# FFN input projection by a seven-product block scheme, with each engine's work in a written order

## The chip, the cores and the metric

The kernel runs on one NeuronCore of a Trainium2 chip. Five engines run side by side, each with its own instruction queue: TensorE (PE in the profile; its weight loads are listed as PEld), VectorE (DVE), ScalarE (ACT), GpSimd (POOL) and SyncE (SP, which here only issues transfers). TensorE multiplies a stationary 128x128 block with a moving block of up to 512 columns and writes to PSUM, which has 8 banks of 128x512 floats. Everything else lies in SBUF. [...]

The metric is device time in microseconds of one execution. A profiled execution gives the trace; its span runs from the first to the last instruction.

## What is computed

One decoder layer on 512 tokens with model width 1024: a hybrid mixer (short gated convolution, stick-breaking attention, a chunked state-space scan, merged by gates), then a SwiGLU FFN with hidden width 2816. Both have a pre-norm conditioned by `c`, and a post-norm with a gate. The part that is changed is the product with `w_ffn_in`:

```
x  = x + gate1 * RMSNorm_post(mixer(h))
h2 = rms_norm(x, g_pre_ffn) * (1 + scale2) + shift2      # 512 x 1024
gt, up = split(h2 @ w_ffn_in, 2)                         # w_ffn_in: 1024 x 5632
f  = (silu(gt) * up) @ w_ffn_out                         # w_ffn_out: 2816 x 1024
x  = x + gate2 * RMSNorm_post(f)
```

All inputs and the output are float32.

## The kernel before

Every large product is done in three matmuls on two parts: an operand is cast to a high part on ACT, and DVE subtracts it from the original to get the low part (`split`, lines 146 to 148; in the profile L147 is the cast, L148 the subtraction). `mm3` (lines 150 to 153) then adds high x high, high x low and low x high into one PSUM bank.

Weights come through a common queue. `chunks` lists all weight blocks of the program in their order of use; `load_chunk` loads the next one on the SP queue into one of three 1 MB tiles (tag `wraw`), and `split_piece` splits 128x1024 of it into a high tile `whi` and a low tile `wlo`, of which there are four each. One such split is a "piece". `piece()` (line 212) hands out piece i and, before that, emits the splits up to piece i+2 (`LOOK = 3`). So the split of a piece stands two pieces ahead of its use in the instruction order.

The program runs through these stages. A start stage makes the modulation and the first projection columns. Then TensorE goes through the mixer's projections, with generators for attention, scan and modulation rows pumped between the pieces. Mixer tiles come from one pool of 41 buffers of 128x512 floats (tag `t2`). Then the output projection `w_o` in two passes of two token blocks each; behind each block `x1_chain` (lines 986 to 1009) does the post-norm, the residual sum and the next pre-norm, and `h2_tiles` transposes the result on TensorE and splits it into `h2h` and `h2l` (8 row blocks of 128 by 512 tokens).

FFN-in (lines 1041 to 1073) goes over 22 blocks of 128 hidden columns, each with a gate half and an up half. A half is one piece: 8 row blocks x 3 matmuls of 512 tokens into one bank. The first four halves are done for tokens 0 to 255 first, while the chain of the last two token blocks still runs, then for tokens 256 to 511. After each block `sigm` (three ACT operations: exp, log, exp) and two DVE products give f, which is split into `fh` and `fl` at once. FFN-out then goes over the 11 pairs of hidden blocks, twice, once for each half of the output columns.

The order of instructions is left to a scheduler outside the start stage; inside a `tc.manual_schedule` block the named engines do their work in the order in which it is written.

The lines that the steps of the prediction touch are `piece` and `split_piece` (weights), lines 1049 to 1073 (FFN-in), 1086 to 1106 (FFN-out) and the tile pools.

## Time and profile before

| | us |
|---|---|
| median of 3 runs (802.52 to 804.99) | 802.79 |
| profiled execution | 804.18 |
| its span | 802.5 |
| TensorE busy | 772.6 |
| DVE busy | 460.8 |
| ACT busy | 376.0 |
| POOL busy | 134.8 |

The difference between the profiled execution and its span is what lies before the first and after the last instruction. Busy times of matmuls overlap in the trace, since they are pipelined: the time that a matmul really takes in a stream is the distance from one start to the next. The clock that the throttle granted to TensorE was full throughout (mean 0.999). In a line of the groups, the columns after the bar are the busy time of the group, the mean duration of one instruction in nanoseconds, and the idle time just before its instructions with what ended it. In a table of stretches each line has the stretch, its length, then busy time and instruction count of PE, PEld, DVE, ACT and POOL, the granted clock, the DMA share and GB/s. FFN-in begins at 426.3 us of the span, FFN-out at 672.9.

### The profile page before, as it was taken

To read this page: it belongs to the slowest core of one execution; us is meant where nothing else is said; L and a number is where in the kernel's file an instruction comes from. 1 tells how busy PE (TensorE), PEld (TensorE's weight loads), DVE (VectorE), ACT (ScalarE), POOL (GpSimd) and SP (SyncE) were. 2 spreads that over 40 slices of the span, in tenths; PEclk is the share of its full clock that TensorE was granted. 3 is DMA by queue.
4 is the path that set the end of the run, shared out by engine and by line. 5 is a ranking of instruction groups with operands and counts; after the bars stand their busy time and mean duration, and the time that the engine had idled before them with its cause. 6 is when DMAs were issued, how large, how long until landed. Compare 5 with 4: busy or idle time off the path is not lost.

```text
span 802.5 us, 9537 instructions
## 1 busy us (share of the span) xinstructions
PE 772.6 (96%) x3661; PEld 631.4 (79%) x3661; DVE 460.8 (57%) x667; ACT 376.0 (47%) x623; POOL 134.8 (17%) x175
## 2 busy tenths in 40 slices
PE   3899999999999999999999999999999999999997
PEld 2679887767678888888778988888888888888886
DVE  5999968568847566545698534434434346323214
ACT  5566544566667374551565634434434444213112
POOL 4453412345520100202133000000000000000000
PEclk9999999999999999999999999999999999999999
DMA  9981441122416686755754332222233345532102
GB/s 281 299 261 55 128 135 53 53 81 94 141 56 203 213 237 208 212 182 121 273 187 129 105 99 70 96 94 72 97 105 105 105 158 186 180 108 92 39 1 105
DMA packets 90525, 108.71 MB, mean 135 GB/s; under 512 B 3244, under 2 KB 69856, under 8 KB 90480
## 3 DMA queue, kind: packets, MB, share of 16 engines
q1 hardware_dynamic: 86128, 99.62, 38.7%
q0 software_dynamic: 3584, 7.42, 4.3%
q10 hardware_dynamic: 768, 1.07, 0.4%
q8 instruction: 28, 0.46, 0.2%
q14 instruction: 17, 0.14, 0.1%
HBM read 102.33 MB, written 2.10 MB: 130 GB/s over the span
## 4 chain that ended last, share of the span: by engine, by line
PE 46%; DVE 4%; issue 1%; ACT 1%; DMA 1%; DVEq 0%; ACTq 0%; POOLq 0%
PE pfg L152 5%; PE pfu L152 5%; PE pfu L151 5%; PE pfg L151 5%; PE pfu L153 4%; PE pfg L153 4%; PE pfo L153 4%; PE pfo L152 4%; PE pfo L151 4%; DVE wlo L148 2%; DVE t2k L997 1%; DVE x L999 1%; DMA gate<-gate 1%; DVE st L1004 1%; PE pf L151 1%
## 5 line engine op out<-in xcount | busy, mean ns | idle before, releaser
L147 ACT CAST whi<-wraw 128x1024 fp32r<-128x1024 f32 (+1 forms) x133 | 137.2, 1035 | 262.0 <-PE pfg L152 76.4
L148 DVE TENSOR_TENSOR wlo<-wraw,whi 128x1024 fp32r<-128x1024 f32 (+1 forms) x133 | 164.9, 1243 | 155.6 <-ACT whi L147 155.1
L152 PE MATMUL pgt<-hl,whi 128*128 128x512 f32 x192 | 75.7, 394 | 0.0
L153 PE MATMUL pgt<-hh,wlo 128*128 128x512 f32 x192 | 75.5, 393 | 0.0
L151 PE MATMUL pgt<-hh,whi 128*128 128x512 f32 x192 | 75.4, 393 | 0.0
L152 PE MATMUL pfg<-h2l,whi 128*128 128x512 f32 x160 | 63.0, 394 | 0.0
L152 PE MATMUL pfu<-h2l,whi 128*128 128x512 f32 x160 | 63.0, 394 | 0.0
L151 PE MATMUL pfg<-h2h,whi 128*128 128x512 f32 x160 | 62.7, 392 | 0.0
L151 PE MATMUL pfu<-h2h,whi 128*128 128x512 f32 x160 | 62.7, 392 | 0.0
L153 PE MATMUL pfu<-h2h,wlo 128*128 128x512 f32 x160 | 62.1, 388 | 0.0
L153 PE MATMUL pfg<-h2h,wlo 128*128 128x512 f32 x160 | 62.1, 388 | 0.0
L152 PE MATMUL pfo<-wlo,fh 128*128 128x512 f32 x154 | 60.8, 395 | 0.0
L153 PE MATMUL pfo<-whi,fl 128*128 128x512 f32 x154 | 60.8, 395 | 0.0
L151 PE MATMUL pfo<-whi,fh 128*128 128x512 f32 x154 | 60.7, 394 | 0.0
L923 POOL DMA_DIRECT2D macc<-in_mod_b_dram x8 | 6.8, 849 | 288.6 <-DVE macc L917 241.5
L917 DVE SCALAR_TENSOR_TENSOR macc<-wraw,sc,macc 128x512 f32<-128x512 f32 x56 | 44.2, 789 | 12.1 <-DMA wraw<-in_mod_w_dram 5.5
L151 PEld LDWEIGHTS pgt<-hh,whi 128*128 128x128 f32 x192 | 36.1, 188 | 8.4 <-issue 0.4
L152 PEld LDWEIGHTS pgt<-hl,whi 128*128 128x128 f32 x192 | 36.1, 188 | 8.1
L153 PEld LDWEIGHTS pgt<-hh,wlo 128*128 128x128 f32 x192 | 36.1, 188 | 7.9
L151 PEld LDWEIGHTS pfu<-h2h,whi 128*128 128x128 f32 x160 | 30.0, 188 | 7.0
L151 PEld LDWEIGHTS pfg<-h2h,whi 128*128 128x128 f32 x160 | 30.0, 188 | 7.0
L153 PEld LDWEIGHTS pfu<-h2h,wlo 128*128 128x128 f32 x160 | 30.0, 188 | 6.7
(360 smaller groups left out, 1668.8 us busy)
## 6 DMA issues: line engine op xcount, KB each, us to landing
wraw<-in_w_ffn_in_dram SPq DMA_DIRECT2D x22, 1024.0 KB, 5.0
wraw<-in_w_in_dram SPq DMA_DIRECT2D x20, 1024.0 KB, 5.2
wraw<-in_mod_w_dram SPq DMA_DIRECT2D x16, 1024.0 KB, 5.2
wraw<-in_w_ffn_out_dram SPq DMA_DIRECT2D x10, 1024.0 KB, 4.9
wraw<-in_mod_w_dram SPq DMA_DIRECT2D x16, 512.0 KB, 6.6
wraw<-in_w_o_dram SPq DMA_DIRECT2D x8, 1024.0 KB, 5.6
gate<-gate POOLq DMA_DIRECT2D x14, 256.0 KB, 4.2
xn<-in_x_dram SPq DMA_DIRECT2D x8, 256.0 KB, 5.0
```

The costliest lines, as they stand in the source:

```text
L147: act.copy(hi, src)
L148: vec.tensor_tensor(lo, src, hi.bitcast(F32), ALU.subtract)
L151: pe.matmul(o, whi, xhi, start=start, stop=False)
L152: pe.matmul(o, whi, xlo, start=False, stop=False)
L153: pe.matmul(o, wlo, xhi, start=False, stop=stop)
L917: vec.scalar_tensor_tensor(acc, mw[:, r], c_, acc, op0=ALU.mult, op1=ALU.add)
L923: nc.gpsimd.dma_start(acc[0:1, :], mod_b[n0:n0 + 512].unsqueeze(0), accum_op=ALU.add)
L997: vec.scalar_tensor_tensor(t_, pos[hf], st[:, 2:3], G1[hf], op0=ALU.mult, op1=ALU.mult)
L999: vec.tensor_tensor(xv, xv, t_, ALU.add)
L1004: vec.tensor_tensor(st[:, 3:4], st[:, 3:4], st[:, 4:5], ALU.add)
```

## The change

FFN-in is done on blocks. The 1024 inner rows are cut in two halves, the tokens in two halves (0 to 255, 256 to 511), and two neighbouring hidden blocks form a unit, of which there are 11. That gives a 2x2 by 2x2 block product, which is computed in seven block products ("steps" 1 to 7) in place of eight. A step multiplies one 512-row, two-halves-wide weight block (gate and up, a piece of 128x1024) with 256 tokens: 2 x 4 x 3 = 24 matmuls of 256 columns. Steps 1 and 2 use weight blocks of the first hidden block with the two inner halves of tokens 0 to 255; steps 7 and 4 use blocks of the second hidden block with token differences; steps 5, 6 and 3 use weight sums. Step 2 adds onto the bank of step 1, step 3 onto that of step 5.

- Weight sums: one DVE sum (`wsum`) and two accumulating DMAs on POOL's queue for the steps 5, 6 and 3, and a third accumulating DMA that changes the weight block of step 7 in place. Each moves 512 KB from SBUF to SBUF.
- Token sums T1 to T4 and their splits are made once, between the steps of the first two units, whose steps are interleaved (1 1 2 2 5 5 6 6 7 7 4 4 3 3). The other nine units go 5 1 4 6 7 2 3.
- Results are combined on DVE and ACT: a copy of step 1's bank, one sum after step 6, three operations `c2` after step 7, one sum in `third_of` after step 3; then the sigmoids and products. The products of a sigmoid are put off to the next step (`later`, `flush`).
- TensorE, DVE and ACT do all this in the written order.
- f is kept unsplit; only unit 0 is split inside FFN-in, unit 1 at its end, the others inside the first half of FFN-out, two units ahead of their use.
- The weights of FFN-in come in columns of 128 (runs of 512 bytes, before 1 KB), into four tiles: the three of before and one more that lies in the memory of the closed mixer pool.
- The pool `t2` shrinks from 41 to 30 buffers. A new pool of 12 buffers (`q2`) holds the branch results of attention and convolution (`ybh`, `ybl`, `yah`, `yal`), the scan's `cbm`, later the rows `SH` and `SC` and the normalised `xm`, and in FFN-in the split token sums `tx`.

```diff
-NT2 = 41
+NT2 = 30
...
+    tq = tqs.enter_context(tc.tile_pool(name="tq", bufs=1, side="right"))
+
+    def q2(name, dt=F32):
+        return tq.tile([P, 512], dt, tag="q2", name=name, bufs=12)
...
+    NU = MF // 2
+    WINO = [(u, q) for q in (1, 2, 5, 6, 7, 4, 3) for u in range(2)]
+    WINO += [(u, q) for u in range(2, NU) for q in (5, 1, 4, 6, 7, 2, 3)]
+    units = {}
+    late_pool = {}
+
+    def wino_load(u, i):
+        at["wino"] = at.get("wino", 0) + 1
+        if at["wino"] % 4:
+            raw = raw_tile()
+        else:
+            raw = late_pool["fp"].tile([P, 2048], F32, tag="raw4", name="wraw", bufs=1)
+        raw = raw.rearrange("p (g k n) -> p g k n", g=2, k=8)
+        for g in range(2):
+            c0 = g * FFN + (2 * u + i) * P
+            nc.sync.dma_start(raw[:, g], w_ffn_in[:, c0:c0 + P].rearrange(
+                "(k p) n -> p k n", k=8))
+        units[u][i] = [raw[:, :, 4 * a:4 * a + 4].rearrange("p g k n -> p g (k n)")
+                       for a in range(2)]
+
+    def wino_piece(u, q):
+        if u not in units:
+            units[u] = {}
+            for i in range(1 if u == 1 else 2):
+                wino_load(u, i)
+        un = units[u]
+        if q == 5:
+            un["s"] = late_pool["fx"].tile([P, 2, 512], F32, tag="wsum", name="wsum", bufs=2)
+            vec.tensor_tensor(un["s"], un[1][0], un[1][1], ALU.add)
+            nc.gpsimd.dma_start(un[1][0], un[0][0], accum_op=ALU.add)
+        src = {1: (0, 0), 2: (0, 1), 4: (1, 1), 7: (1, 0)}.get(q)
+        src = un[src[0]][src[1]] if src else un["s"]
+        hi = wp.tile([P, 1024], FR, tag="whi", name="whi").rearrange("p (g n) -> p g n", g=2)
+        lo = wp.tile([P, 1024], FR, tag="wlo", name="wlo").rearrange("p (g n) -> p g n", g=2)
+        split(hi, lo, src)
+        if q in (5, 6):
+            nc.gpsimd.dma_start(un["s"], un[0][q - 5], accum_op=ALU.add)
+        return [t_.rearrange("p g (k n) -> p g k n", k=4) for t_ in (hi, lo)]
...
-    for mp in range(MF // 2):
-        chunks.append(("cols", [[(0, KD, w_ffn_in[:, o + mp * 256:o + (mp + 1) * 256])]
-                                for o in (0, FFN)], 256, 2))
+    chunks.append(("wino", WINO, 0, 1))
...
-    pf = {}
-    fw = {}
-    for i in range(4):
-        pf[i], fw[i] = bank("pf"), piece()
-        ffn_mm(pf[i], fw[i], lo_t, True, False)
-        if i == 2:
-            h2_tiles(*todo.pop(0))
-    h2_tiles(*todo.pop(0))
...
-        if m < 2:
-            pg, pu = pf[2 * m], pf[2 * m + 1]
-        else:
-            pg, pu = bank("pfg"), bank("pfu")
-            for pt in (pg, pu):
-                ffn_mm(pt, piece(), all_t, True, True)
-        f = fq.tile([P, T], F32, tag="f", name="f")
-        sigm(f, pg)
-        vec.tensor_tensor(f, f, pg, ALU.mult)
-        vec.tensor_tensor(f, f, pu, ALU.mult)
-        split(fh[:, m, :], fl[:, m, :], f)
...
+    fp = ctx.enter_context(tc.tile_pool(name="fp", bufs=1, reuse_waits="tile"))
+    fxs = ExitStack()
+    fx = fxs.enter_context(tc.tile_pool(name="fx", bufs=1, reuse_waits="tile"))
+    late_pool.update(fp=fp, fx=fx)
+    wino_load(1, 1)
...
+    def flush():
+        while later:
+            later.pop(0)()
+    def step(q, o, start, stop):
+        hi, lo = piece()
+        flush()
+        for g in range(2):
+            cs = slice(g * 256, g * 256 + 256)
+            for k in range(4):
+                if q in tb_of:
+                    xh, xl = hbh[:, tb_of[q], k, :], hbl[:, tb_of[q], k, :]
+                else:
+                    xh, xl = (t_[k // 2][:, k % 2, :] for t_ in tx[q])
+                for part, (a_, b_) in enumerate(((hi, xh), (hi, xl), (lo, xh))):
+                    pe.matmul(o[:, cs], a_[:, g, k, :], b_,
+                              start=(start and g + k + part == 0),
+                              stop=(stop and k == 3 and part == 2), skip_group_check=True)
+    def gated(dst, g, u, sg):
+        sigm(sg, g)
+        def products():
+            vec.tensor_tensor(dst, sg, g, ALU.mult)
+            vec.tensor_tensor(dst, dst, u, ALU.mult)
+        later.append(products)
...
+    def gated_m1(f4, p4, p5, p7, u2):
+        c2 = two(temp("c2", 1024))
+        vec.tensor_tensor(c2[:, 0, :], p7, u2, ALU.add)
+        vec.scalar_tensor_tensor(c2[:, 1, :], p5, -1.0, c2[:, 0, :], op0=ALU.mult,
+                                 op1=ALU.subtract)
+        vec.tensor_tensor(c2[:, 0, :], p4, c2[:, 0, :], ALU.subtract)
+        gated(two(f4[:, 1, :]), c2[:, :, 0:256], c2[:, :, 256:512], two(temp("sg1", 512)))
+    def third_of(f4, p5, u2):
+        vec.tensor_tensor(u2, p5, u2, ALU.add)
+        gated_m0(f4, u2, 1)
...
+    with tc.manual_schedule(engines={ET.PE, ET.DVE, ET.Activation}):
+        pb_ = {1: [], 5: [], 6: [], 7: [], 4: []}
+
+        def fresh(q):
+            pb_[q].append(bank(f"pf{q}"))
+            step(q, pb_[q][-1], True, True)
+        u2s = [temp("u2", 512, 2) for _ in range(2)]
+        for u in range(2):
+            fresh(1)
+            act.copy(u2s[u], pb_[1][u])
+        for u in range(2):
+            step(2, pb_[1][u], False, True)
+            pts[u] = h2_tr(*todo.pop(0))
+
+        t1_, b22, t2_, t3_, t4_ = (f4_tile(n) for n in ("t1r", "b22", "t2r", "t3r", "t4r"))
+
+        def k4(t_, u):
+            return t_[:, u, :].rearrange("p (k t) -> p k t", k=4)
+
+        def parts_of(q, t_, u):
+            for k0 in (0, 2):
+                ts = slice(u * P, (u + 1) * P)
+                h_, l_ = (t__[k0 // 2][:, :, ts] for t__ in tx[q])
+                split(h_, l_, k4(t_, u)[:, k0:k0 + 2, :])
+        for q in (6, 7, 4):
+            tx[q] = [[q2("tx", FR).rearrange("p (k t) -> p k t", k=2) for _ in range(2)]
+                     for _ in range(2)]
+        tks = [slice(u * P, (u + 1) * P) for u in range(2)]
+        for u in range(2):
+            vec.tensor_tensor(k4(t1_, u), hbh[:, 0, :, tks[u]].bitcast(F32), pts[u][0],
+                              ALU.subtract)
+            vec.tensor_tensor(k4(t1_, u), k4(t1_, u), hbl[:, 0, :, tks[u]].bitcast(F32), ALU.add)
+            split(hbh[:, 3, :, tks[u]], hbl[:, 3, :, tks[u]], k4(t1_, u))
+            act.copy(k4(b22, u), pts[u][1])
+        for u in range(2):
+            vec.scalar_tensor_tensor(k4(t2_, u), k4(t1_, u), -1.0, k4(b22, u), op0=ALU.mult,
+                                     op1=ALU.subtract)
+            parts_of(6, t2_, u)
+        for u in range(2):
+            f4s.append(f4_tile("f4"))
+            gated_m0(f4s[u], pb_[1][u], 0)
+            flush()
+        fresh(5)
+        fresh(5)
+        for u in range(2):
+            vec.tensor_tensor(k4(t3_, u), k4(b22, u), pts[u][0], ALU.subtract)
+            parts_of(7, t3_, u)
+        for u in range(2):
+            fresh(6)
+            vec.tensor_tensor(u2s[u], pb_[6][u], u2s[u], ALU.add)
+        for u in range(2):
+            vec.tensor_tensor(k4(t4_, u), hbh[:, 1, :, tks[u]].bitcast(F32), k4(t2_, u), ALU.add)
+            vec.tensor_tensor(k4(t4_, u), k4(t4_, u), hbl[:, 1, :, tks[u]].bitcast(F32), ALU.add)
+            parts_of(4, t4_, u)
+            split(hbh[:, 2, :, tks[u]], hbl[:, 2, :, tks[u]], k4(b22, u))
+        fresh(7)
+        fresh(7)
+        for u in range(2):
+            fresh(4)
+            gated_m1(f4s[u], pb_[4][u], pb_[5][u], pb_[7][u], u2s[u])
+        for u in range(2):
+            step(3, pb_[5][u], False, True)
+            third_of(f4s[u], pb_[5][u], u2s[u])
+        for u in range(2, NU):
+            f4s.append(f4_tile("f4"))
+            p5 = bank("pf5")
+            step(5, p5, True, True)
+            p1, u2 = bank("pf1"), temp("u2", 512, 2)
+            step(1, p1, True, True)
+            act.copy(u2, p1)
+            p4 = bank("pf4")
+            step(4, p4, True, True)
+            p6 = bank("pf6")
+            step(6, p6, True, True)
+            vec.tensor_tensor(u2, p6, u2, ALU.add)
+            p7 = bank("pf7")
+            step(7, p7, True, True)
+            gated_m1(f4s[u], p4, p5, p7, u2)
+            step(2, p1, False, True)
+            gated_m0(f4s[u], p1, 0)
+            if u == NU - 1:
+                t_ = fp.tile([P, 2, 2, T], FR, tag="raw4", name="fparts", bufs=1)
+                f_parts(0, (t_[:, 0], t_[:, 1]))
+            step(3, p5, False, True)
+            third_of(f4s[u], p5, u2)
+        flush()
+    fxs.close()
+    tqs.close()
+    fo = ctx.enter_context(tc.tile_pool(name="fo", bufs=1, reuse_waits="tile"))
+
+    def f_split(u):
+
+        f_parts(u, [fo.tile([P, 2, T], FR, tag="f4o", name="fparts", bufs=10) if u < 6
+                    else f4_tile("fparts", FR) for _ in range(2)])
+    f_split(1)
...
             w = piece()
+            if hf == 0:
+                f_split(i + 2)
```

84 lines of the change are left out of this document (53 added, 31 removed).

## The prediction

> **What bounds the kernel now.** I read the page first: busy shares, the row of slices, the granted clock, the chain that ended last.
>
> ```profile
> PE 772.6 (96%) x3661; PEld 631.4 (79%) x3661; DVE 460.8 (57%) x667; ACT 376.0 (47%) x623; POOL 134.8 (17%) x175
> ...
> PE   3899999999999999999999999999999999999997
> ...
> PEclk9999999999999999999999999999999999999999
> ...
> PE 46%; DVE 4%; issue 1%; ACT 1%; DMA 1%; DVEq 0%; ACTq 0%; POOLq 0%
> ```
>
> TensorE is full from the second slice to the last at an unthrottled clock, and the chain runs through it. So matmul columns are the currency, and a change that removes columns gains as long as VectorE (DVE) and ScalarE (ACT) still deliver operands in time. The second view is the table of stretches: the two mixer stretches, then the start of FFN-in, its steady part, and the first half of FFN-out.
>
> ```profile
> 45.00:200.00 155.00, 152.00 (x779) 123.44 (x778) 123.62 (x215) 91.47 (x167) 62.31 (x90) 1.00 0.33 103
> 200.00:380.00 180.00, 178.37 (x795) 142.79 (x794) 110.08 (x145) 95.99 (x147) 33.30 (x37) 1.00 0.59 176
> ...
> 426.30:453.20 26.90, 25.56 (x210) 24.61 (x209) 20.48 (x26) 15.34 (x34) 6.31 (x4) 1.00 0.25 79
> 453.20:672.90 219.70, 219.70 (x962) 180.30 (x961) 93.32 (x107) 90.40 (x122) 0.82 (x1) 1.00 0.34 110
> 672.90:738.00 65.10, 65.10 (x280) 52.20 (x280) 26.53 (x33) 17.66 (x25) 1.97 (x3) 1.00 0.38 120
> ```
>
> FFN-in is 426.3 to 672.9, 246.6 us. Its steady part is 960 matmuls of 512 columns in 219.7 us, 0.2289 us each, with DVE busy 93 and ACT 90: both wait for TensorE. One pair of hidden blocks (a "unit" below, 96 such matmuls) costs 21.97 us.
>
> **TensorE work removed.** The seven products need 11 units x 7 steps x 24 = 1848 matmuls of 256 columns. The start of FFN-in already has that shape, from the timeline:
>
> ```profile
> 446.27 0.28 PE L153 MATMUL pf<-h2h,wlo 128*128 128x256 f32 x1
> ...
> 447.21 0.28 PE L152 MATMUL pf<-h2l,whi 128*128 128x256 f32 x1
> ```
>
> Eight intervals lie between these starts: 0.94/8 = 0.1175 us each, slightly over half of 0.2289. A step is 2.82 us, a unit 19.74, all 1848 matmuls 217.1. Today's are 219.7 + 192 x 0.1175 = 242.3. TensorE alone would save 25.2 us. The matmul record of 0.28 us says that a result lands 0.16 us behind the issue.
>
> **What the other engines get.** The page's groups by shape, DVE first:
>
> ```profile
> L148 DVE TENSOR_TENSOR wlo<-wraw,whi 128x1024 fp32r<-128x1024 f32 x129 | 161.7, 1256 | 155.6 <-ACT whi L147 155.1 <-PE pk L153 0.4
> L1071 DVE TENSOR_TENSOR f<-f,pfg 128x512 f32<-128x512 f32 x20 | 13.8, 689 | 17.0 <-ACT f L159 17.0
> L774 DVE TENSOR_TENSOR ce<-ce,xs 128x256 f32<-128x256 f32 x8 | 3.3, 411 | 0.0
> L147 ACT CAST whi<-wraw 128x1024 fp32r<-128x1024 f32 x129 | 134.8, 1048 | 262.0 <-PE pfg L152 76.4 <-PE pfu L152 48.0 <-PE pfo3b L153 31.0
> L158 ACT ACTIVATE f<-f,one_c 128x512 f32<-128x512 f32 x22 | 15.9, 724 | 0.7
> L159 ACT ACTIVATE f<-f 128x512 f32<-128x512 f32 x22 | 13.9, 632 | 0.7
> L157 ACT ACTIVATE f<-pfg 128x512 f32<-128x512 f32 x20 | 11.9, 593 | 0.0
> L585 ACT ACTIVATE sb_e<-sb_e,one_c 128x256 f32<-128x256 f32 x2 | 1.0, 506 | 0.0
> L584 ACT ACTIVATE sb_e<-sb_e 128x256 f32<-128x256 f32 x2 | 0.8, 416 | 0.0
> L583 ACT ACTIVATE sb_e<-pz 128x256 f32<-128x256 f32 x2 | 0.8, 384 | 0.0
> L280 ACT CAST wxh<-wxr 128x256 fp32r<-128x256 f32 x8 | 3.2, 400 | 1.0 <-DMA wxr<-in_w_in_dram 1.0
> ```
>
> Per unit DVE gets seven weight subtractions and one weight sum (8 x 1.26), seven operations of 512 (7 x 0.69) and four of 256 (4 x 0.41): 16.5 us, against four subtractions and six of 512, 9.2 us, in 21.97 now. ACT gets seven casts (7.3), one copy (0.6), a sigmoid of 512 (0.59 + 0.72 + 0.63 = 1.95) and two of 256 (0.38 + 0.51 + 0.42 = 1.31 each): 12.5 us. DVE would be at 84% of a 19.74 us unit. That fits as a sum, but the order is fixed on both engines, and ACT and DVE feed each other: cast, then subtraction; PSUM sum on DVE, then sigmoid on ACT, then products on DVE. So I follow the cycle of waits.
>
> How far instructions of one engine overlap, and what a hand-over costs, from the timeline:
>
> ```profile
> 387.28 4.72 DVE L148 TENSOR_TENSOR wlo<-wraw,whi 128x1024 fp32r<-128x1024 f32 x4
> ...
> 461.02 0.63 ACT L159 ACTIVATE f<-f 128x512 f32<-128x512 f32 x1
> ...
> 461.69 0.69 DVE L1071 TENSOR_TENSOR f<-f,pfg 128x512 f32<-128x512 f32 x1 [0.69 <-ACT f L159]
> ```
>
> Four subtractions take 4.72 instead of 5.02, and a hand-over is 461.69 - 461.65 = 0.04.
>
> **Steady unit (steps 5, 1, 4, 6, 7, 2, 3).**
> - Loop part 1, from the last matmul of step 7 to the split of the next unit's piece 5. On DVE the three c2 operations (2.07); behind them on ACT the sigmoid of 512 (1.95), and only then the cast of piece 5 (1.05); then its subtraction (1.26). With 0.16 of drain and four hand-overs 6.65 us. TensorE has steps 2 and 3 meanwhile plus the two matmuls that need no low part, 5.88. It waits 0.8.
> - Part 2, from there to the split of piece 4. DVE does two products of 512, the subtraction of piece 1, two products of 256 and the sum of third_of, 4.15. ACT can cast piece 4 only behind third_of's sigmoid (1.31 + 1.05), then the subtraction (1.26); with hand-overs 7.89. TensorE has the rest of step 5, step 1 and two matmuls, 5.65. It waits 2.2.
> - Part 3: the rest of step 4, steps 6 and 7, 8.23 of pure TensorE.
>
> The loop is 22.8, less about 0.4 for overlap on DVE: 22.4 us, already 0.4 above today's unit.
>
> The third accumulating DMA can lengthen it. It may start only once piece 6 is split, 2.08 after part 2 (two products, one subtraction); after it come cast and subtraction of piece 3 (2.43 with hand-overs), and the c2 operations stand behind that subtraction on DVE. So a landing time D is free up to 8.39 - 4.51 = 3.9 us. No transfer of 512 KB from SBUF to SBUF is in the trace; the nearest are these, the second of them giving minimum, median and maximum:
>
> ```profile
> gate<-gate POOLq DMA_DIRECT2D x14, 256.0 KB, 4.2
> ...
> DMA to landing us min/median/max: 3.3/4.2/7.1
> ...
> wraw<-in_w_ffn_out_dram SPq DMA_DIRECT2D x10, 1024.0 KB, 4.9
> ...
> wraw<-in_w_ffn_out_dram SPq DMA_DIRECT2D x2, 512.0 KB, 4.1
> ```
>
> Bounds for D are 3.3 (the fastest of half the size) and 8.4 (twice the median). Doubling a load adds 0.8; for an accumulation, which reads its target too, I take 1.0 and D = 5.2, nearest to the median row. That adds 1.3: a unit of 23.7. Nine units against 21.97: +15.6 us; with D at its ends +4 and +44.
>
> [...]
>
> **The first two units.** They interleave (1 1 2 2 5 5 6 6 7 7 4 4 3 3), and the token sums T1 to T4 are formed on the way. Step 5 waits for the last transposes, which the x1 chain sets:
>
> ```profile
> 440.22 1.32 PE L1015 MATMUL pt<-ident,xm 128*128 128x128 f32 x8 [1.32 <-DVE xm L1007]
> ...
> 441.55 0.74 PE L151 MATMUL pf<-h2h,whi 128*128 128x256 f32 x4
> ```
>
> From 441.55 TensorE has ten steps, 28.2 us. DVE has some 30 operations of 512, 20 of 256 and nine of 1024: 20.7 + 8.2 + 11.3 = 40.2. It also stands for the casts of T1 and of every second part (about 3.6) and for two sigmoids that share one buffer (2.6). So this part is bound by DVE: about 46.4 after 441.55, or 61.7 after 426.3, against 26.9 + 21.97 = 48.9 now: +12.8. Its bounds: 0 (full overlap, T1 of the first half done earlier, no waits: 33.5) and +18 (another 5 us if the piece-5 splits wait for the x1 chain on DVE or for the fourth weight tile, which lies in memory of the closed pool).
>
> **What I cost at nothing.** In FFN-out ten splits of 1024 columns come in, 12.6 on DVE and 10.5 on ACT; in its first half they are busy 26.5 and 17.7 of 65.1 us, so TensorE covers them; without cover the first one costs up to 2 us. The last unit needs no next piece 5, which I leave in. The weight loads are the same bytes in shorter runs, at a DMA share of 0.34. In the mixer 12 long-lived tiles leave a pool that shrinks by 11; TensorE idles 3.0 + 1.6 us there now, and I take 0, within 3 either way.
>
> **Sum.** +15.6 + 12.8 = +28.4. The profiled execution took 804.18 us (span 802.5, 1.7 around it); the median of the runs is 802.79, 1.4 lower. Forecast 804.2 + 28.4 = 832.6 on its scale, 831 on the median's. Its own range is +4 to +62, 807 to 865.
>
> **Rivals.**
> - The queues keep up everywhere and TensorE stays the bound: -25.2, 778. For it: both engines have slack as sums. Against it: parts 1 and 2 are chains of single instructions, each with a row. Chance 0.14.
> - Only the start stalls and the steady units run at 19.74: 12.8 - 9 x 2.23 = -7.3, 795. It needs piece 5 split 3 us sooner than I find. Chance 0.11.
> - The accumulating DMAs collide with the 1 MB loads that the freed tiles start: D = 8.4, 44 + 12.8 = +57, 860. The maximum of 7.1 for half the size speaks for it; the third DMA mostly falling ahead of the loads speaks against. It decides from D = 3.9 on. Chance 0.11.
> - The mixer loses more to its smaller pool than FFN-in changes by: if its idle of 4.6 us tripled, +9 on the forecast, 840. Chance 0.04.
> - My forecast: 0.60.
>
> Below 0.3% (2.4 us) a change cannot be told from none here. Faster gets the first two rivals: 0.24, a little less for their upper edge; same 0.07 from the edges where gains and stalls cancel; slower 0.69. The range 784 to 857 leaves out about half of each outer rival and the forecast's thin top.
>
> **What would show it.** A steady unit of 22 to 25 us between the starts of its step 5, with TensorE idle before steps 5 and 4, released by wlo or whi; DVE above 65% in FFN-in; casts of wsum waiting for a DMA; the two first units ending near 488. If TensorE is solid from 450 on and a unit is 19.7, I am wrong in parts 1 and 2; if whi waits for the accumulation by over 3 us, D was too small.

## The result, and the profile after

The changed kernel takes 869.53 us (median; 867.97 to 870.63) against 802.79 (802.52 to 804.99): a ratio of 1.0823, with a 95% interval of 1.0798 to 1.0849. The forecast was 831 with a range of 784 to 857. The sign was right, the size was not: 28.4 us were forecast and 66.7 came, above the range.

First the page of the changed kernel: busy shares, TensorE's slices and granted clock, and the chain that ended last, by engine and by line.

```profile
PE 779.5 (90%) x4357; PEld 664.8 (77%) x4357; DVE 558.7 (64%) x801; ACT 421.6 (49%) x703; POOL 173.0 (20%) x208
...
PE   4899999999999999999859688788888888899997
...
PEclk9999999999999999999988999999999999999999
...
PE 12%; DMA 12%; DVE 7%; issue 7%; ACT 4%; DVEq 0%; ACTq 0%; POOLq 0%
DMA wsum<-wraw 9%; PE pfo L159 3%; PE pfo L160 3%; PE pfo L158 3%; DVE wlo L155 3%; ACT whi L154 2%; PE pf L1135 2%; DMA wraw<-in_mod_w_dram 2%; DMA macc<-in_mod_b_dram 1%; DVE macc L974 1%; ACT sg L165 1%; DVE fparts L155 1%; DVE c L1159 1%; DVE c L1160 1%; ACT sg L164 1%
```

TensorE was solid before; now the slices from the 21st to the 34th, which are FFN-in, show 5 to 9 and mostly 8, and the first two of them run below full clock. The chain, 46% TensorE before, is a mixture, and its largest line is a transfer that did not exist before: the accumulation onto wsum. The table of stretches of the changed kernel gives the four parts: the mixer from 385 (up to there the two kernels run level), the first two units, the nine steady units, FFN-out. Columns: stretch and length, then busy time and instruction count of PE, PEld, DVE, ACT and POOL, granted clock, DMA share, GB/s.

```profile
385.00:431.40 46.40, 42.08 (x173) 33.19 (x173) 35.32 (x43) 26.79 (x52) 7.87 (x5) 0.93 0.60 196
431.40:499.74 68.34, 49.78 (x354) 47.84 (x352) 49.99 (x71) 31.24 (x62) 15.39 (x11) 0.88 0.57 123
499.74:732.00 232.26, 194.32 (x1512) 185.40 (x1512) 142.54 (x177) 108.60 (x159) 32.38 (x28) 0.98 0.67 143
732.00:868.90 136.90, 128.08 (x598) 104.67 (x598) 61.50 (x75) 41.63 (x63) 1.59 (x2) 0.97 0.30 104
```

The same stretches of the kernel before, where they were not shown yet (its FFN-in is 426.3 to 672.9):

```profile
385.00:426.30 41.30, 39.01 (x173) 30.65 (x172) 33.08 (x40) 26.47 (x50) 8.59 (x5) 1.00 0.59 210
...
672.90:802.50 129.60, 123.91 (x599) 102.32 (x598) 44.09 (x55) 30.04 (x50) 1.97 (x3) 0.99 0.29 94
```

So the 66.4 us by which the spans differ (868.9 - 802.5) lie here:

| part | before | after | forecast change | measured change |
|---|---|---|---|---|
| up to FFN-in | 426.3 | 431.4 | 0 | +5.1 |
| first two units | 48.9 | 68.3 | +12.8 | +19.4 |
| nine steady units | 197.7 | 232.3 | +15.6 | +34.6 |
| FFN-out to the end | 129.6 | 136.9 | 0 | +7.3 |
| sum | 802.5 | 868.9 | +28.4 | +66.4 |

The view of TensorE's waits over all of FFN-in, 431.4 to 732 (waiting line and releaser: us in total, times, longest), tells what the matmuls waited for:

```profile
PE pf L1135 <- ACT whi L154: 15.4, 18, 3.5
PE pf L1135 <- DVE wlo L155: 15.3, 21, 0.8
PE pf L1135 <- DVE c L1160: 11.8, 9, 2.3
```

In the steady units the first two rows are the waits ahead of steps 5 and 4 that were forecast, high half first, low half behind. The third row is a wait ahead of step 3: once in the first two units, and once each in eight of the nine steady ones.

### The profile page after: what moved, and what is told of

It reads as the page before. It is cut to its first block, busy times and chain, and to the rows that moved or that the text cites. A ratio compares the mean times of both kernels' runs of the same rounds, so it can differ in the third digit from the quotient of the medians.

```text
span 868.9 us, 11371 instructions
## 1 busy us (share of the span) xinstructions
PE 779.5 (90%) x4357; PEld 664.8 (77%) x4357; DVE 558.7 (64%) x801; ACT 421.6 (49%) x703; POOL 173.0 (20%) x208
## 5 line engine op out<-in xcount | busy, mean ns | idle before, releaser
L1135 PE MATMUL pf<-hbh,whi 128*128 128x256 f32 x352 | 102.9, 292 | 28.7 <-DVE c L1160 11.8
L1135 PE MATMUL pf<-tx,whi 128*128 128x256 f32 x528 | 101.0, 293 | 8.9 <-ACT whi L154 8.9
L1135 PE MATMUL pf<-hbh,wlo 128*128 128x256 f32 x352 | 101.7, 289 | 7.4 <-DVE wlo L155 7.4
L1135 PE MATMUL pf<-hbl,whi 128*128 128x256 f32 x352 | 100.9, 287 | 0.1
L1135 PEld LDWEIGHTS pf<-hbh,whi 128*128 128x128 f32 x352 | 68.6, 195 | 32.6 <-issue 13.3
L1135 PEld LDWEIGHTS pf<-tx,whi 128*128 128x128 f32 x528 | 84.8, 197 | 10.8 <-ACT whi L154 10.7
L1135 PE MATMUL pf<-tx,wlo 128*128 128x256 f32 x264 | 77.6, 294 | 8.0 <-DVE wlo L155 7.9
L1135 PEld LDWEIGHTS pf<-hbh,wlo 128*128 128x128 f32 x352 | 68.8, 195 | 9.5 <-DVE wlo L155 9.5
L1135 PEld LDWEIGHTS pf<-hbl,whi 128*128 128x128 f32 x352 | 68.9, 196 | 0.5 <-DVE hbl L155 0.4
L158 PE MATMUL pfo<-whi,fparts 128*128 128x512 f32 x154 | 62.3, 405 | 5.5 <-ACT fparts L154 5.5
L154 ACT CAST whi<-wsum 128x1024 fp32r<-128x1024 f32 x33 | 34.2, 1040 | 66.7 <-DMA wsum<-wraw 61.0
L160 PE MATMUL pfo<-whi,fparts 128*128 128x512 f32 x154 | 61.9, 406 | 0.3 <-DVE fparts L155 0.3
```

Source lines behind the costliest of these rows:

```text
L154: act.copy(hi, src)
L158: pe.matmul(o, whi, xhi, start=start, stop=False)
L160: pe.matmul(o, wlo, xhi, start=False, stop=stop)
L1135: pe.matmul(o[:, cs], a_[:, g, k, :], b_, start=(start and g + k + part == 0), stop=(stop and k == 3 and part == 2), skip_group_check=True)
```

## The experiments on a steady unit

The timeline of one steady unit of the changed kernel shows where the third row comes from (start, length, instruction; in brackets the idle time before it and its releaser).

```profile
564.77 1.20 POOL L274 DMA_DIRECT2D wsum<-wraw  x1 [8.28 <-DVE wlo L155]
...
571.10 1.05 ACT L154 CAST whi<-wsum 128x1024 fp32r<-128x1024 f32 x1 [6.49 <-DMA wsum<-wraw]
...
572.18 1.23 DVE L155 TENSOR_TENSOR wlo<-wsum,whi 128x1024 fp32r<-128x1024 f32 x1 [3.13 <-ACT whi L154]
...
573.32 0.68 DVE L1159 TENSOR_TENSOR c<-pf,u 128x512 f32<-128x512 f32 x1
...
574.88 0.36 PE L1135 MATMUL pf<-hbh,whi 128*128 128x256 f32 x1 [0.89 <-DVE c L1160]
```

The third accumulating DMA of the unit in order of time (the first is the one for step 7, the second and the third go onto wsum) is issued at 564.77. ScalarE has nothing else to do and stands 6.49 us for it; VectorE stands another 3.13 in front of the subtraction, and only behind that begin the three c2 operations, at 573.32. Their data were there earlier: step 2 ran the 2.82 us before TensorE's idle 0.89, so step 7 had ended by 574.88 - 0.89 - 2.82 = 571.17. The second c2 operation reads the bank that step 3 adds to, so TensorE waits too. From issue to cast are 6.3 us, where I had used D = 5.2.

**Without the third DMA, and without any.** Both kernels leave out terms of the weight sums, so their products are incomplete; they serve for the time alone.

```diff
-        if q in (5, 6):
+        if q == 5:
             nc.gpsimd.dma_start(un["s"], un[0][q - 5], accum_op=ALU.add)
```

> The changed kernel without the third accumulating transfer of each unit: the weight sum of step 3 lacks its last term, so that product is left incomplete. Theory (that transfer, landing 6.0 us after its issue against 3.9 free in the loop that I worked out, holds back cast and subtraction of piece 3, behind which the c2 operations stand on VectorE): the loop falls to parts 1 to 3 alone, 22.4 to 22.6 us, the idle time before step 3 released by the c2 read goes to about 0, the whole is some 20 us shorter, 849 us. Rival (the transfer is hidden behind the sigmoids and products, and the idle time only moves to the next split): the unit stays within 0.5 us of 25.1, 865 us or more.

```diff
-            nc.gpsimd.dma_start(un[1][0], un[0][0], accum_op=ALU.add)
...
-        if q in (5, 6):
-            nc.gpsimd.dma_start(un["s"], un[0][q - 5], accum_op=ALU.add)
```

> The changed kernel without any of the three accumulating transfers: steps 5, 6 and 3 multiply with the first weight sum alone, so those products are left incomplete. Theory (only the third transfer is on the path): the same unit as without the third alone, 22.4 to 22.6 us, within 5 us of it in all; the first block of two units may gain 0 to 6 us, since its splits of pieces 5 and 6 wait for two transfers. [...]

Measured: 850.17 us without the third (1.058, 1.0559 to 1.0601) and 847.55 without all three (1.0548, 1.0527 to 1.0569), both as the theory had it. The unit is read from VectorE's weight sum, which comes once a unit. The row of the timeline in the changed kernel (first and last start):

```profile
L266 DVE TENSOR_TENSOR wsum<-wraw x5: 1215/1216/1216, 550.6 to 650.9; 128x1024 f32<-128x1024 f32 x5
```

and in the kernel without the third DMA, with its two longest kinds of wait of TensorE:

```profile
L266 DVE TENSOR_TENSOR wsum<-wraw x6: 1212/1215/1215, 545.2 to 658.3; 128x1024 f32<-128x1024 f32 x6
```

```profile
PE pf L1135 <- DVE wlo L155: 14.3, 22, 0.8
PE pf L1135 <- ACT whi L154: 10.3, 10, 3.5
```

That is 100.3/4 = 25.1 us a unit against 113.1/5 = 22.62. The loop without that transfer is what I had worked out (22.4); the other two accumulations are off the path, since without them a unit is 22.63 too (but for one of 24.2), and the nine units together take 211.8 us against 211.5. The third costs 2.5 us a unit. The waits for whi and wlo before steps 5 and 4 stay; of those for c2 one is left in all of FFN-in, 2.3 us long.

**The c2 operations ahead of piece 3's split.** The transfer stays; only what is queued behind it on VectorE and ScalarE changes: with the new last argument the split of piece 3 is issued behind the c2 operations, ahead of the sigmoid.

```diff
-            step(7, p7, True, True)
-            gated_m1(f4s[u], p4, p5, p7, u2)
+            step(7, p7, True, True, LOOK - 1)
+            gated_m1(f4s[u], p4, p5, p7, u2, True)
```

> The changed kernel with one thing moved in each steady unit: the split of piece 3 is written behind the three c2 operations and ahead of their sigmoid, where the changed kernel has it ahead of them. The three accumulating transfers stay. Theory (the third transfer costs what it does only because c2 stands behind the split of piece 3 on VectorE, so a late landing holds up c2, the sigmoid, the cast of the next piece 5 and so the whole loop): the unit falls from 25.1 us to my loop without the transfer, 22.4 to 23.0, like the run that left the transfer out (22.64), and the whole to 849 to 853 us; TensorE may wait 0.7 us before step 3 for the low part. Rival (the transfer itself is late for step 3 in any order): the unit stays at 24 or more, 862 us or more, with TensorE waiting before step 3 for the cast of piece 3.

Measured: 858.23 us (1.0676, 1.0631 to 1.0721). In the steady units, by the same row of the timeline:

```profile
L266 DVE TENSOR_TENSOR wsum<-wraw x5: 1218/1218/1219, 546.6 to 639.0; 128x1024 f32<-128x1024 f32 x5
```

92.4/4 = 23.1 us. So 2.0 of the 2.5 us come back with the transfer as it was: what cost was not its landing time as such but that c2 stood behind it. The whole kernel misses its 849 to 853: at the start of FFN-out TensorE now waits 6.5 us where it waited 3.3. From this kernel's waits of TensorE:

```profile
PE pfo L158 <- ACT fparts L154: 6.5, 1, 6.5
```

**The steady units in another order.** The same instructions of the nine units are emitted from one sorted list: each step at its place, every other operation at a written position counted in steps from the unit's step 5. In the list sp5 is the split of step 5's weights, cp the copy, c2 the three operations on PSUM, s and p a sigmoid and its products.

```diff
+        pos = {'wsum': -2.92, 'sp5': -2.01, 'sp1': -1.12, 'sp4': -0.06, 'sp6': 0.99, 'sp7': 1.33, 'sp2': 1.85, 'cp': 2.99, 'u2a': 4.83, 'sp3': 4.96, 'c2': 5.54, 'sm0': 5.95, 'sm1': 5.96, 'pm0': 5.99, 'th': 8.56, 'pm1': 9.09, 'sh': 9.72, 'ph': 10.62}
```

> The changed kernel with the nine steady units re-emitted in a software-pipelined order: the weight sum and the splits of pieces 5 and 1 stand two or three steps ahead of the unit, the splits of 4, 6 and 7 one step earlier than now against the steps, the split of piece 3 just ahead of the c2 operations, and the second and third sigmoid with their products overlap the next unit. Same instructions, same transfers, same first two units. Theory (the loss of the steady units is the written order: splits that stand behind sigmoids and products, and a c2 read that stands behind the split of piece 3): a unit falls from 25.1 us to 19.5 to 20.5, nine units give back 40 to 50 us, 820 to 830 us in all, TensorE idle before steps 5 and 4 under 0.3 us per unit. Rival (VectorE's load of 16.5 us with its stalls, or the three accumulating transfers of 6.0 us one after another, set the unit): the unit stays at 22.5 or more, 846 us or more.

Measured: 837.2 us (1.0414, 1.0394 to 1.0433), between the two theories. The row of the weight sum in this kernel (its helper has moved by a line), and two rows of its page on the accumulating DMAs (count, KB, median us to landing):

```profile
L265 DVE TENSOR_TENSOR wsum<-wraw x9: 1217/1218/1220, 499.2 to 669.2; 128x1024 f32<-128x1024 f32 x9
```

```profile
wsum<-wraw POOLq DMA_DIRECT2D x22, 512.0 KB, 7.0
...
wraw<-wraw POOLq DMA_DIRECT2D x11, 512.0 KB, 8.0
```

170.0/8 = 21.25 us, within 1.5 us of TensorE's 19.74. In the nine units (502.45 to 707.11) the waits for whi and wlo have shrunk to 2.2 and 2.0 us; the largest kind that is left is the one for c2:

```profile
PE pf L1144 <- DVE c L1173: 11.5, 6, 4.4
```

In this list too c2 is written behind the split of piece 3 (sp3 at 4.96, c2 at 5.54), and that split still stands for the third transfer: ScalarE's casts of wsum wait 53.7 us for transfers in this kernel, in all. The transfers take longer here than in the changed kernel, whose page gives:

```profile
wsum<-wraw POOLq DMA_DIRECT2D x22, 512.0 KB, 6.0
...
wraw<-wraw POOLq DMA_DIRECT2D x11, 512.0 KB, 5.2
```

The order was most of the loss in the steady units: 25.1 to 21.25 with nothing removed.

## The experiments on the first two units

The timeline of the changed kernel through this part, TensorE and VectorE:

```profile
441.97 0.58 PE L1135 MATMUL pf<-hbh,whi 128*128 128x256 f32 x1 [4.75 <-ACT u L1184]
...
445.59 1.22 DVE L266 TENSOR_TENSOR wsum<-wraw 128x1024 f32<-128x1024 f32 x1
...
452.55 0.68 DVE L1204 TENSOR_TENSOR t1r<-hbh,pt 128x512 f32<-128x512 f32 x1
...
457.35 0.58 PE L1135 MATMUL pf<-hbh,whi 128*128 128x256 f32 x1 [5.72 <-ACT hbh L154]
```

TensorE first waits 4.75 us for the copy of a bank on ScalarE. In ScalarE's order that copy, at 441.36, stands directly behind the last squares of the x1 chain, at 440.75; its target also lies in a pool that is opened once the mixer's pool is closed. Which of the two held it, no run separates. Then the weight sums and both piece-5 splits stand ahead of the first token sum T1 on VectorE, from 445.59 to 452.55, and step 5 waits 5.72 for T1's cast. The clock is throttled in this part as well; a stretch of the changed kernel, granted clock in the third column from the right:

```profile
440.00:448.00 8.00, 6.03 (x34) 6.03 (x35) 4.79 (x8) 4.60 (x10) 3.49 (x3) 0.60 0.49 131
```

At a granted clock of 0.50, from 440 to 444, the records of the matmuls behind that wait are 0.41 us long (the first 0.58) and their starts lie 0.21 us apart; from 446.54 on they are 0.28 long and 0.12 apart. To see whether the clock or VectorE's order costs the time, 151 matmuls into an unread bank were put where TensorE waits, 125 of them in this part, so that it stays busy.

```diff
+        def warm(n):
+            o = bank("pdum")
+            for i in range(n):
+                pe.matmul(o[:, 0:256], hbh[:, 0, 0, 0:P], hbh[:, 0, 0, :], start=i == 0,
+                          stop=i == n - 1, skip_group_check=True)
...
+            warm(36)
             step(2, pb_[1][u], False, True)
```

> The changed kernel with 151 extra matmuls of 256 columns into a bank that nobody reads, put in TensorE's order where it idled 2 us and more from 437 to 496 us and before FFN-out (36 before the first step 2, 44 before the first step 5, 27 before the first step 4, 18 before the first step 3, 26 before FFN-out), each a little less than the idle time, so that TensorE has work there. Theory of the clock (the half-clock stretches behind these idle times are what made the first block 6.6 us longer than my 61.7): the granted clock stays full there, the first block ends 5 us or more sooner, the whole is 5 to 9 us shorter. Rival (the first block is bound by VectorE, and a slower TensorE only waits less afterwards): the granted clock recovers just the same, but the first block ends within 1.5 us of where it did, and the whole is within 3 us of 869.5.

Measured: 867.63 us (1.0793, 1.0748 to 1.0838), within 3 us of the changed kernel, as the rival had it. The stretch of this kernel:

```profile
434.63:502.20 67.57, 59.87 (x478) 58.27 (x476) 50.00 (x71) 31.25 (x62) 15.42 (x11) 0.97 0.58 125
```

The clock is nearly full again (0.97; 1.00 from 440 to 448), and the part still takes 67.57 us against 68.34. The throttled clock there is a follow-up of the waiting, not its cause: in the changed kernel the first throttled step loses some 2 us (20 intervals of 0.21 us in place of 0.12), and the 5.72 us of waiting for T1 behind it take them up. What VectorE's order costs is shown below by the kernels that write out the order of this part too.

## The experiments on the mixer and on FFN-out

**The pools alone.** The kernel before, with only the mixer's tiles divided over two pools as the change does; FFN-in stays as it was.

```diff
-NT2 = 41
+NT2 = 30
...
+    def q2(name, dt=F32):
+        return tq.tile([P, 512], dt, tag="q2", name=name, bufs=12)
```

> The kernel before with only the change of the pools: the 12 long-lived mixer tiles in a pool of their own, the old pool at 30 buffers; FFN as before. Theory (the pools cost nothing; the 5.1 us by which FFN-in of the changed kernel starts later come from the work that is written behind the mixer's end): within 0.3% of 802.8. Rival (the smaller pool of 30 holds the mixer back): 805.5 to 808, with idle time of TensorE before 426 us released by tiles of those pools.

Measured: 807.24 us (803.29 to 809.83), 1.0041 with 1.0026 to 1.0057: some 3.3 us, as the rival had it. If all of it falls in the mixer, it is the larger part of the 5.1 us lost there. Its profiled execution was the fastest of the ten and shows nothing of the loss, so neither the place nor the mechanism is shown. Nor is the 5.1 a fixed amount: in the kernels of the experiments above and below that keep the changed kernel's mixer, FFN-in begins between 429.0 us (without all three DMAs) and 434.6 (with the extra matmuls). What the changed kernel's own profile shows in that place is a throttled clock: the last matmul ahead of it in the timeline, and the stretch.

```profile
387.54 0.50 PE L159 MATMUL pwo<-wlo,mh 128*128 128x512 f32 x1 [1.73 <-DVE wlo L155]
```

```profile
388.00:392.00 4.00, 4.00 (x13) 3.10 (x12) 3.50 (x4) 1.90 (x3) 0.00 (x0) 0.57 1.03 381
```

The kernel before waits 1.21 us at the same matmul and keeps a full clock:

```profile
386.82 0.50 PE L152 MATMUL pwo<-wlo,mh 128*128 128x512 f32 x1 [1.21 <-DVE wlo L148]
```

**FFN-out.** Ten splits of hidden blocks come in the stretch that loses 7.3 us. The timeline of the changed kernel shows TensorE waiting for such splits, once just ahead of this stretch and once in it:

```profile
732.00 0.50 PE L158 MATMUL pfo<-whi,fparts 128*128 128x512 f32 x1 [3.32 <-ACT fparts L154]
...
741.60 0.50 PE L158 MATMUL pfo<-whi,fparts 128*128 128x512 f32 x1 [2.19 <-ACT fparts L154]
```

Two edits, the second on top of the first: the splits of hidden units 0 and 1 are made inside the last steady unit, ahead of its step 5 and behind its c2 operations, and then the last gate rows, whose casts also run on ScalarE, begin two pieces later.

```diff
+            if u == NU - 1:
+                t_ = fp.tile([P, 2, 2, T], FR, tag="raw4", name="fparts", bufs=1)
+                f_parts(0, (t_[:, 0], t_[:, 1]))
...
+                f_parts(1, [fp.tile([P, 2, T], FR, tag="wsum", name="fparts", bufs=2)
+                            for _ in range(2)])
...
-    f_split(1)
```

> The changed kernel with the first two hidden parts for FFN-out written earlier: those of unit 0 ahead of the last unit's step 5, those of unit 1 behind its c2 operations, in the two weight-sum buffers that are free by then. All else stays. Theory (FFN-in's last unit ran 28.9 us against 24.8, and FFN-out 7.3 us longer than before, because these casts stand behind the last unit's sigmoids on ScalarE): the 3.3 and 2.2 us of TensorE's idle time released by the hidden parts at the start of FFN-out go, with the half-clock stretches behind them, 6 to 10 us in all, 860 to 864. Rival (ScalarE and VectorE only do the same work earlier and the last unit gets longer by it): less than 3 us, 867 or more.

```diff
-                if i == 0:
+                if i == 2:
                     sides.append(mods_in_turn([(5, hf) for hf in range(2)], False, mah_late))
```

> The run with the earlier hidden parts (all else as in the changed kernel), with the same step: the rows of the last modulation gate begun two pieces later. Theory: FFN-out, 7.3 us longer in the changed kernel than before, falls to 130 to 132 (from 132 in the run before), 861 to 864 in all. Rival: no change within 1 us, since there TensorE waited 1.48 us for that cast and kept its clock.

Measured: 864.59 us (1.0754, 1.0735 to 1.0773), then 861.09 (1.0716, 1.0698 to 1.0735). The stretch of FFN-out in the first and in the second:

```profile
730.81:862.90 132.09, 124.72 (x598) 102.45 (x598) 62.22 (x76) 42.77 (x66) 1.83 (x3) 1.00 0.33 114
...
728.64:859.50 130.86, 125.00 (x598) 103.05 (x598) 62.66 (x76) 43.19 (x66) 1.85 (x3) 0.99 0.34 115
```

FFN-out takes 136.9 us in the changed kernel, 132.1 and 130.9 here, and 129.6 in the kernel before. So 6.0 of its 7.3 us came from the place of these splits and of the gate rows on ScalarE, not from the splits' amount; and the work was not merely moved into the steady units, which take 232.2 us with the first edit and 232.3 without. By the medians the two edits bring 4.9 and 3.5 us; the second part is more than the stretch shows.

## Versions with the whole of FFN-in in a written order

If orders were most of it, then a kernel with the same products and a better order over the first two units, the nine steady ones and the passage to FFN-out should come near the kernel before, or below it. All of FFN-in was put into one sorted list, as above, with the first splits of FFN-out in it.

```diff
+        first = [
...
+            (1.879, 'wsum', 1), (2.5, '2', 0), (3.171, 'cp', 1), (3.5, 'tr', 0), (3.625, 'T1', 0),
+            (3.958, 'sp5', 1), (4.5, '2', 1), (5.171, 'b22', 0), (5.246, 'T2', 0), (5.5, 'tr', 1),
...
+        ev = list(first)
+        for u in range(2, NU):
+            ev += [(16 + 7 * (u - 2) + k_ + 0.5, q_, u) for k_, q_ in enumerate("5146723")]
+            ev += [(16 + 7 * (u - 2) + x_, n_, u) for n_, x_ in steady.items()
+                   if not any(f_[1:] == (n_, u) for f_ in first)]
```

The versions differ in who forms the third weight sum, and in the positions; those shown are the last kernel's.

**The DMA forms it, as in the change.**

> The reordering of the steady units carried to the rest of FFN-in: same matmuls, sums, splits and transfers as the changed kernel, in a new written order on TensorE, VectorE and ScalarE for the first block of two units too (the copies of step 1's banks, the token sum T1 and the split of piece 5 ahead of what they stood behind), and the splits of the first FFN-out weights and of the first hidden block put before the end of FFN-in. Theory (the written order is what cost most): first block 52 to 56 us in place of 68.3, a steady unit 20 to 21.5, FFN-out begins 55 to 65 us sooner than in the changed kernel, 800 to 815 us in all. Rival (accumulating transfers that take 7 to 8 us each, as they did in the run with reordered steady units, bind at this pace): unit 21.5 to 23, 818 to 830.

Measured: 818.43 us (1.0175, 1.0147 to 1.0203). The two parts of FFN-in in this kernel:

```profile
429.17:488.49 59.32, 46.90 (x353) 45.75 (x351) 51.85 (x73) 31.31 (x61) 18.82 (x12) 0.88 0.71 154
488.49:674.11 185.62, 178.52 (x1491) 177.47 (x1490) 132.63 (x167) 107.19 (x154) 30.02 (x25) 0.99 0.77 170
```

The two first units lose 9.0 us of their 68.3, with the same operations, but miss the 52 to 56 of the theory; a steady unit is 20.6 in the mean of nine, as the theory had it, and the whole is in the rival's range. VectorE is busy 51.85 of the 59.32 us, so the first part is near the limit that the amount of its work sets.

**GpSimd forms it.**

```diff
-        if q in (5, 6):
+        if q == 5:
             nc.gpsimd.dma_start(un["s"], un[0][0], accum_op=ALU.add)
+        if q == 6:
+            pool.tensor_tensor(un["s"], un["s"], un[0][1], ALU.add)
```

> As the run before it in this list (full reordering, slightly other positions), with the third sum of each unit made by an addition of 128x1024 on GpSimd in place of the third accumulating transfer. By the row of 128x512 on GpSimd (1.85 us) the addition should take about 3.7 us, against 7 to 9 from issue to landing. Theory (the late third transfer is what is left): unit 19.7 to 20.3, first block as in the run before it, 785 to 800 us in all, below the kernel before. Rival (GpSimd's additions and VectorE's operations slow each other, with VectorE at some 80 per cent): VectorE's subtraction of 128x1024 rises over 1.35 us, the unit stays above 21, 812 or more.

Measured: 811.46 us (1.0091, 1.0072 to 1.011), between the theory's 785 to 800 and the rival's 812. The steady units take 182.1 us, 20.2 each, as the theory had it; the loss is elsewhere, in the first two (61.1) and at the start of FFN-out, where TensorE waits 6.0 us once. The slowing of VectorE that the rival named came all the same. A subtraction on VectorE beside nothing takes 1.21 us in this kernel (at 468.79); these are GpSimd's addition and the two subtractions beside it:

```profile
534.45 2.39 POOL L281 TENSOR_TENSOR wsum<-wsum,wraw 128x1024 f32<-128x1024 f32 x1 [1.33 <-DVE wlo L155]
...
534.62 4.44 DVE L155 TENSOR_TENSOR wlo<-wraw,whi 128x1024 fp32r<-128x1024 f32 x2 [0.26 <-ACT whi L154]
```

The two take 4.44 us instead of about 2.4: the addition is not free for VectorE.

**VectorE forms it**, as an event s3 of the list with its own position, in two sets of positions, and the first hidden blocks are split earlier.

```diff
-            pool.tensor_tensor(un["s"], un["s"], un[0][1], ALU.add)
...
+            vec.tensor_tensor(units[u]["s"], units[u]["s"], units[u][0][1], ALU.add)
```

> As the run with the third sum on GpSimd, but that sum is made by a VectorE addition of 128x1024 (1.22 us), since the GpSimd addition of 2.39 us stretched the VectorE subtraction beside it from 1.22 to 3.29 us; and the parts of the second and third hidden pair for FFN-out are written inside the ordered block, ahead of the FFN-out weight casts that wait for their transfer, with the positions of the first block shifted. Theory: steady unit 19.7 to 19.9 (VectorE at 17.7 of it), FFN-out's second piece waits under 1 us in place of 6.0, first block 1 to 2 us shorter, 798 to 805 in all. Rival (VectorE's added 1.2 us per unit or the block's end costs what is gained): 808 or more.

> The same with other positions of the first block's splits, copies and token sums (the copies of step 1's banks and the sums T1 in another order against the first piece-5 splits). Theory (the first block is bound by the sum of VectorE's work, some 44 us behind the x1 chain, and not by its order any more): within 2 us of the run before it. Rival (the order still decides): more than 3 us apart, by the stretch from the first step 1 to the first steady step 5.

Measured: 802.59 us (0.9988, 0.997 to 1.0005) and 804.1 (0.9994, 0.9971 to 1.0017). Neither can be told from the kernel before. In the first, the first two units take 58.3 us and the nine 180.2. That two quite different orders come out within 2 us of each other, as the theory had it, speaks for VectorE's amount of work as the limit of the first two units; it does not prove it.

**FFN-out's weight splits one piece later, then the gate rows two pieces later.**

```diff
-            w = piece()
+            w = piece(LOOK if hf or i > 2 else LOOK - 1)
```

> The second of the two runs with the third sum on VectorE, with one more step in FFN-out: in its first three pieces the weight splits are written one piece later, so that the cast of a weight chunk that lands at about 680 us no longer stands ahead of the last unit's sigmoid and of the hidden parts on ScalarE (it held them 3.6 us, and TensorE 2.3). Theory: TensorE waits under 1 us in that stretch, 2 to 4 us less in all, 799 to 802, below the kernel before (803.7) by 0.2 to 0.6 per cent. Rival (the hidden parts are then late for another reason, VectorE being busy 17 of the first 17.1 us of FFN-out): 803 to 805, the same as the kernel before.

Measured: 804.32 us (1.001, 0.9988 to 1.0033): no gain, as the rival had it. At the start of FFN-out TensorE's wait for a hidden block's cast falls from 2.3 to 0.3 us; in its place, at 704.92, it waits 3.06 us for a gate row's cast.

Hence the last kernel, with the edit that was shown for the gate rows on top:

> The run with the reordered FFN-in, third sum on VectorE and later weight splits, with one more step: in FFN-out's first half the two rows of the last modulation gate are begun two pieces later. In the run before, FFN-out took 136.6 us against 129.6 in the kernel before; TensorE stood 3.06 us at 704.9 us before the first row product, released by the cast of the second row's sum, and ran at half clock for about 7 us behind that. Theory (that wait and the half clock are what is left of FFN-out's loss): FFN-out 130 to 131, 797 to 800 in all, ratio to the kernel before 0.992 to 0.995. Rival (the transfers of the modulation weights, which share the three weight tiles, only move the wait to a weight piece): 803 or more.

Measured: 801.46 us (798.73 to 804.18) against 803.35 of the kernel before on the same chip, 0.9975 with 0.996 to 0.9989. That lies between the theory's 797 to 800 and the rival's 803. It is a quarter of a per cent below the kernel before, less than the 0.3% that the prediction took as the least to be told; the interval leaves out 1, but this is the sixth of the written orders that were tried. The stretches of this kernel:

```profile
428.26:486.86 58.60, 47.44 (x353) 46.58 (x352) 52.80 (x72) 32.55 (x63) 14.57 (x10) 0.85 0.60 135
486.86:665.53 178.67, 178.67 (x1516) 178.67 (x1514) 152.71 (x184) 107.65 (x153) 19.75 (x17) 1.00 0.69 157
665.53:798.70 133.17, 124.89 (x600) 102.96 (x598) 62.18 (x78) 44.33 (x69) 2.77 (x4) 0.99 0.32 107
```

TensorE is busy in all of the 178.67 us of the steady units: 19.85 each, against 19.74 by the count of columns. They gain 197.7 - 178.7 = 19.0 us. The first two units give back 58.6 - 48.9 = 9.7, FFN-out 3.6 and the mixer 2.0: -3.8 in the spans (798.7 - 802.5). So a tenth of FFN-in's matmul columns, 25.2 of 242.3 us, ends as 2 us of time.

What is left in the first two units is partly what was there before. From this kernel's view of TensorE's waits:

```profile
PE pf L1156 <- ACT u L1252: 6.6, 1, 6.6
...
PE pf L1156 <- ACT hbh L154: 1.7, 1, 1.7
```

The wait for T1's cast has fallen from 5.7 to 1.7 us (with 2.0 more for its low part), while the wait for the copy of a bank has grown from 4.75 to 6.6. No written order removed that one: in the six its longest is 5.5 to 6.7 us.

## Why the prediction was wrong

The terms of the sum that failed, by the share of the missing 38.0 us (66.4 - 28.4): D 10.2, the edges of the steady part 8.7, VectorE's waits in the first two units 6.6, and the zeros for FFN-out and the mixer 7.3 and 5.1. TensorE's saving and the loop without the transfer were right.

- **TensorE's work removed: right.** 19.85 us a unit where it alone decides, against 19.74.
- **Loop parts 1 to 3 of the steady unit: right.** 22.4 us worked out, 22.62 measured without the third DMA. The waits lay where they were put, ahead of steps 5 and 4. The chain of single instructions decided, not the sum of busy time. The sign "DVE above 65% in FFN-in" did not come: 64% over all of FFN-in, 61% in the steady units.
- **The term D, the third accumulating DMA: the mechanism right, the size off.** The view of the tile wsum has landing times of

```profile
DMA to landing us min/median/max: 5.0/6.0/8.3
```

  and with the cast's start it was 6.3 us in the unit shown. 6.3 - 3.9 gives +2.4 instead of +1.3, and 2.5 was measured. On seven units of 25.16 us (527.57 to 703.7) this and the 0.2 above make 10.2 of the missing 38.0 us. The 1.0 us that I took for doubling an accumulation was an estimate: the medians are 4.2 us for 256 KB (the gate row of the kernel before) and 6.0 for 512 KB here. My own test, whi waiting for the accumulation by over 3 us, came true (6.49).
- **"Nine units" was a steady number times nine: the edges failed.** The first takes 27.8 us and the last 28.3, 8.7 more than two at 23.7. The first runs at a granted clock of 0.72 between 506 and 512; the last contains the 3.32 us of waiting for FFN-out's operands. What makes up the rest of the 8.7 stays open: with that wait gone, in the first edit on FFN-out, the nine units took as long as before.
- **The first two units: VectorE's work right, its waiting too small.** +19.4 against +12.8, with +18 as the upper bound. Behind the x1 chain I had summed 40.2 us of VectorE's work and added 6.2 of waits. From its first weight sum there to the first steady step 5 (445.59 to 499.74) VectorE is busy 38.5 us and idle 15.6; the largest part, 8.0, is for the casts of weights on ScalarE. The upper bound's reason, piece-5 splits behind the x1 chain on VectorE, is what the order shows: the first weight sum follows the chain's last operation, at 444.27, directly. That T1 then stands behind those splits, and step 5 behind T1, I had not seen, nor the wait of 4.75 us for the copy. The written orders bring 7 to 10 us back in this part; as they change more than one place, the share of T1 itself stays open.
- **"What I cost at nothing": failed twice.** FFN-out lost 7.3 us and the mixer 5.1. For FFN-out I compared busy sums (26.5 and 17.7 of 65.1) and priced the first split at up to 2 us without cover. A wait of 2.19 us for a hidden block's cast came in it, besides the 3.32 in the unit ahead, and the granted clock fell to 0.79 from 732 to 748; the gate rows' casts on the same engine were not counted. The two edits of places bring 6.0 of the 7.3 back. For the mixer "within 3 either way" was too narrow; the pools by themselves cost 3.3 in all, and why stays open.
- **The rivals.** None of them came as it stood. The collision of DMAs gave 860 by a landing time of 8.4, and that is nearest in time, but its mechanism is not what happened: the median landing is 6.0.

The granted clock was no part of my sum. In the changed kernel the length of a wait alone does not decide whether it drops: behind the wait of 1.73 us at 387.54 it was 0.57 from 388 to 392, while behind this wait of 2.35 us it stayed at 1.00, by the stretch that follows:

```profile
550.13 0.36 PE L1135 MATMUL pf<-hbh,whi 128*128 128x256 f32 x1 [2.35 <-DVE c L1160]
```

```profile
552.00:556.00 4.00, 2.66 (x21) 2.25 (x20) 2.20 (x3) 3.85 (x7) 1.91 (x2) 1.00 0.58 101
```

What decides, the runs do not show.

## What to carry to other kernels

When a change takes work off the engine that is the bound, do not compare busy sums of the others: walk one cycle of the new loop through each in-order queue, and ask of every instruction that waits for a transfer what stands behind it. Do the same for the first and the last round and for the stage behind, which here cost as much as the loop itself. Where a trace shows short waits spread over many lines with no engine full, try another order of the same instructions before giving up the idea; here that alone took the steady unit from 25.1 to 21.25 us, and 66 us of loss became 2 us of gain once the orders of the edges and of FFN-out were changed too and an addition on VectorE stood in place of the third DMA.

## What the hardware showed that I had not expected

- An accumulating DMA of 512 KB within SBUF took 6.0 us (onto wsum, 5.0 to 8.3) and 5.2 (for step 7) in the median, and 7.0 and 8.0 in the kernel with reordered steady units of 21.25 us, three to a unit. The shorter unit alone is not the reason: in the last kernel, with units of 19.85 us and two to a unit, the page has

```profile
wraw<-wraw POOLq DMA_DIRECT2D x11, 512.0 KB, 5.7
wsum<-wraw POOLq DMA_DIRECT2D x11, 512.0 KB, 5.3
```

  What lengthens them where there are three stays open.
- The throttled clock cost next to nothing in the first two units: at a granted clock of 0.97 in place of 0.88 they took 67.57 us in place of 68.34.
- VectorE's subtraction with two operands in SBUF goes from about 1.2 us to 2.2 in the mean of two beside a GpSimd addition of 2.39. The addition ends at 534.45 + 2.39 = 536.84, and the pair ends at 534.62 + 4.44 = 539.06, 2.2 us behind it; two subtractions of 1.21 us (the one at 468.79 in the same kernel) would be about 2.4. A VectorE addition of 128x512 took 2.77 us at 461.50 beside a GpSimd addition of 2.76 (460.95), and 0.69 at 457.77 without one.
